# Two MLP products as seven block products each: one step of a hybrid diffusion backbone on one core

## The chip, the cores and the metric

The kernel runs on one core of a Trainium2 chip, and the metric is the device time of one execution in microseconds (us). Its engines run beside each other and meet through semaphores: TensorE (PE, matrix products), VectorE (DVE), ScalarE (ACT), GpSimd (POOL) and SyncE (SP), whose queue issues all the transfers of this kernel. A smaller time is better.

## The reference, cut to what matters

Two layers run over 1152 tokens (1024 of a sample, 128 of a prompt) with 1024 features. Each layer norms and modulates the tokens, projects them, runs a convolution, grouped attention and neighbourhood attention, projects back, and ends with an MLP:

```python
    x = x + g1 * (jnp.concatenate([a_out, b_out, c_out], axis=-1) @ w_out)
    h = _rms(x, n2) * (1 + sc2) + sh2
    x = x + g2 * (jnp.square(jax.nn.relu(h @ w1)) @ w2)
```

`w1` is 1024 x 4096 and `w2` 4096 x 1024. All is float32. `sh`, `sc` and `g` come from a modulation vector, one for the sample's tokens and one for the prompt's, as `silu(c) @ ada_w + ada_b` for each layer.

## The kernel before

Features lie on partitions, tokens along the free axis. Residuals `X[k]` (k = 0 to 7, 128 features each) and the normed activations stay in SBUF. Nothing is ordered by a scheduler: the code is emitted in the order in which it stands (`tc.manual_schedule()`), generators are advanced by hand with `next`, and each engine runs its own instructions strictly in that order. Helpers record most operations, so that many have the line of a helper: L92 is `tt` (tensor_tensor), L95 `stt` (scalar_tensor_tensor), L86 and L89 ACT's activation and copy, L132 a transfer.

**High and low parts.** PE multiplies in fp32r. To keep float32 accuracy every operand is split: `hi` is the value cast by ACT, `lo` is value minus `hi` by DVE or POOL (`split`). A product is then three matmuls, hi*hi, hi*lo and lo*hi, into one PSUM bank (there are eight, tag `p`).

**The MLP (`mlp`).** The 4096 inner features are 32 blocks `f` of 128, taken two at a time in 16 rounds `c`. A round runs the first product for both blocks, first over the first 512 tokens (`mm1`, L1481 to L1483, 512 columns a matmul), then over the other 640 (`mm1_rest`, through `both_parts` at L1351, 320 columns a matmul). The results go through `relu2` and a split, stay in SBUF as `hid`, and the same round multiplies them with the matching rows of `w2` (`mm2`, L1505 to L1507, 512 columns) and adds each result, times the gate, to `X` by one DVE instruction straight from PSUM. The prompt's part of the second product has the tokens as the stationary side (`mm2p`, L1525 to L1527, names `accp`), with `prompt_tail` at the end.

```python
            for k in range(KT):                                                       # mm1
                mm(ps, wh[:, k, :], h[:, k, :], start=(k == 0), stop=False)           # L1481
                mm(ps, wh[:, k, :], lo[:, k, :], start=False, stop=False)             # L1482
                mm(ps, wl[:, k, :], h[:, k, :], start=False, stop=(k == KT - 1))      # L1483
...
            mm2_part(ps, c, si, n, 1)                                                 # mm2
            stt(xs(n, si), ps, g2[:, 0, n:n + 1], xs(n, si), ALU.mult, ALU.add)
```

So a layer's MLP is 768 matmuls of 512 columns and 1536 of 320 in the first product, 1536 + 192 of 512 in the second.

**Around it.** `out_proj` comes ahead. Its norm for the MLP (`norm2`, names `nx`, `h2h`, `h2l`) runs for the first 512 tokens beside the last parts of the output projection, and for the other 640 beside the MLP's first round. `modulation(0, [1, 2])` is spare work of PE beside layer 0's projections (`fill`, names `aw`, `psmod`, L211); `modulation_beside(1)` makes all six sixths of layer 1's modulation on DVE beside layer 0's MLP (names `macc`), with one small PE sum and four transposes for each sixth (L269, L275). In the last round of layer 0 the next layer's first norm begins. In the last layer finished tokens are turned and stored by `put` (L1616).

## Time and profile before

| | |
|---|---|
| three runs | 3103.09 to 3104.21 us, median 3103.54 |
| profiled execution | span 3103.8 us, within those runs |
| PE / DVE / ACT / POOL busy | 96% / 63% / 35% / 23% of the span |
| TensorE clock granted, mean | 0.984 |
| layer 0's MLP | 749.2 to 1583.2 us of the span |
| layer 1's MLP and the outputs | 2274.5 to 3103.8 us |
| bytes moved | 242.10 MB, mean 78 GB/s |

A row of the profile names line, engine, operation and `out<-in` by the program's names, then shapes as partitions x elements; `busy` of a DVE or POOL instruction contains what it waits inside the instruction. Matmuls overlap their neighbours, so the time that one costs is the distance from its start to the next one's start, not its own duration.

### The profile page before, as it was taken

What the parts mean: (1) busy time and instruction counts of PE and PEld (TensorE: products, weight loads), DVE (VectorE), ACT (ScalarE), POOL (GpSimd) and SP (SyncE); (2) the same over time, 40 slices, a digit from 0 to 9 for tenths busy, and PEclk for the clock granted to TensorE, in tenths of its full rate; (3) what the DMA queues carried; (4) which work ended last, traced back from release to release, by engine and by line L of the source; (5) the groups of instructions that cost most, each with busy time, mean ns of one, the idle gap of its engine ahead of it and who ended that gap; (6) DMA issues with size and microseconds to landing.
All of it is one profiled execution on the core that took longest, in us unless ns stands there. A gap on an engine that the chain in (4) does not pass through costs nothing.

```text
span 3103.8 us, 43730 instructions
## 1 busy us (share of the span) xinstructions
PE 2985.8 (96%) x17136; PEld 2460.4 (79%) x17136; DVE 1962.4 (63%) x3547; ACT 1074.5 (35%) x2230; POOL 718.4 (23%) x653
## 2 busy tenths in 40 slices
PE   6998999999999999999999898999999999999999
PEld 4888645888888888888879884468888888888887
DVE  6587787846766666657467977877374444444444
ACT  4334366844221212121252344578252121212121
POOL 3576256312100000000046754452030000000000
PEclk8999999999999999999999899999999999999999
DMA  7467103331312222222133440134211111111111
GB/s 275 115 183 195 59 16 81 86 95 48 102 60 83 78 78 75 82 62 82 43 109 72 107 120 25 40 75 115 62 41 48 35 48 41 41 41 41 41 48 68
DMA packets 317774, 242.10 MB, mean 78 GB/s; under 512 B 110464, under 2 KB 274048, under 8 KB 316544
## 3 DMA queue, kind: packets, MB, share of 16 engines
q1 hardware_dynamic: 317568, 239.31, 26.2%
q8 instruction: 135, 2.21, 0.3%
q14 instruction: 71, 0.58, 0.1%
HBM read 195.74 MB, written 43.52 MB: 77 GB/s over the span
## 4 chain that ended last, share of the span: by engine, by line
PE 80%; DVE 12%; ACT 3%; POOL 2%; DMA 2%; issue 1%; SPq 1%; DVEq 0%; POOLq 0%; ACTq 0%
PE ps L1351 14%; PE ps L1505 7%; PE ps L1507 7%; PE ps L1506 7%; PE ps L1481 4%; PE ps L1483 4%; PE ps L1482 4%; PE psacc L1149 3%; PE pso L1351 3%; PE pspv L1016 2%; PE pspt L1000 2%; PE pst L573 2%; PE pst L572 2%; PE pst L574 2%; DVE cacc L95 2%; PE psst L1163 2%
## 5 line engine op out<-in xcount | busy, mean ns | idle before, releaser
L95 DVE SCALAR_TENSOR_TENSOR X<-ps,mod,X 128x512 f32<-128x512 f32 x512 | 378.6, 748 | 217.3 <-PE ps L1507 215.4
L86 ACT ACTIVATE re<-ps 128x320 f32<-128x320 f32 (+1 forms) x192 | 87.5, 491 | 1125.9 <-PE ps L1483 853.3
L1505 PE MATMUL ps<-hidh,w2h 128*128 128x512 f32 x1024 | 407.6, 398 | 4.6 <-ACT hidh L89 4.1
L1507 PE MATMUL ps<-hidh,w2l 128*128 128x512 f32 x1024 | 405.0, 396 | 1.1 <-DVE w2l L92 1.1
L1506 PE MATMUL ps<-hidl,w2h 128*128 128x512 f32 x1024 | 405.3, 396 | 0.6 <-DVE hidl L92 0.6
L92 DVE TENSOR_TENSOR re<-ps,re 128x320 f32<-128x320 f32 (+1 forms) x192 | 101.1, 554 | 400.7 <-ACT re L86 400.4
L573 PE MATMUL pst<-wl,hh 128*128 128x256 f32 x1040 | 297.8, 286 | 17.3 <-DVE wl L92 17.3
L572 PE MATMUL pst<-wh,hh 128*128 128x256 f32 x1040 | 298.9, 287 | 2.6 <-ACT wh L89 2.6
L574 PE MATMUL pst<-wh,hl 128*128 128x256 f32 x1040 | 296.2, 285 | 0.0
L92 POOL TENSOR_TENSOR nacc<-nacc,nsq 128x512 f32<-128x512 f32 (+1 forms) x36 | 40.1, 1121 | 930.7 <-ACT nsq L86 930.6
L1505 PEld LDWEIGHTS ps<-hidh,w2h 128*128 128x128 f32 x1024 | 193.4, 189 | 52.7 <-ACT hidh L89 5.0
L1351 PE MATMUL ps<-h2l,w1h 128*128 128x320 f32 x1024 | 233.5, 309 | 0.3 <-POOL h2l L92 0.2
L1351 PE MATMUL ps<-h2h,w1h 128*128 128x320 f32 x1024 | 233.7, 309 | 0.0
L1351 PE MATMUL ps<-h2h,w1l 128*128 128x320 f32 x1024 | 232.7, 308 | 0.0
L1507 PEld LDWEIGHTS ps<-hidh,w2l 128*128 128x128 f32 x1024 | 193.6, 189 | 47.7 <-DVE w2l L92 1.9
L1506 PEld LDWEIGHTS ps<-hidl,w2h 128*128 128x128 f32 x1024 | 193.7, 189 | 44.1 <-DVE hidl L92 1.2
L573 PEld LDWEIGHTS pst<-wl,hh 128*128 128x128 f32 x1040 | 201.1, 193 | 18.2 <-DVE wl L92 18.1
L572 PEld LDWEIGHTS pst<-wh,hh 128*128 128x128 f32 x1040 | 201.0, 193 | 12.6 <-PE pst L574 3.5
L1482 PE MATMUL ps<-h2l,w1h 128*128 128x512 f32 x512 | 201.8, 394 | 1.7 <-POOL h2l L92 1.7
L1481 PE MATMUL ps<-h2h,w1h 128*128 128x512 f32 x512 | 202.7, 396 | 0.0
L1483 PE MATMUL ps<-h2h,w1l 128*128 128x512 f32 x512 | 201.7, 394 | 0.0
L574 PEld LDWEIGHTS pst<-wh,hl 128*128 128x128 f32 x1040 | 201.1, 193 | 0.0
(264 smaller groups left out, 6520.9 us busy)
## 6 DMA issues: line engine op xcount, KB each, us to landing
aw<-in_ada_w SPq DMA_DIRECT2D x160, 256.0 KB, 4.3
w1r<-in_mlp_w SPq DMA_DIRECT2D x64, 512.0 KB, 4.1
w2r<-in_mlp_w SPq DMA_DIRECT2D x64, 512.0 KB, 3.6
ddA<-o SPq DMA_DIRECT2D x144, 128.0 KB, 2.3
wr<-in_w_in SPq DMA_DIRECT2D x28, 512.0 KB, 4.1
qd<-ddA SPq DMA_DIRECT2D x48, 256.0 KB, 3.3
kd<-ddA SPq DMA_DIRECT2D x16, 576.0 KB, 4.8
awh<-in_ada_w SPq DMA_DIRECT2D x8, 1024.0 KB, 12.6
```

What stands on the lines that cost most here:

```text
L92: (eng or nc.vector).tensor_tensor(out=out, in0=a, in1=b, op=op)
L95: nc.vector.scalar_tensor_tensor(out=out, in0=a, scalar=s, in1=b, op0=op0, op1=op1)
L572: mm(o, hi, wh, start=(k == 0), stop=False)
L573: mm(o, hi, wl, start=False, stop=False)
L574: mm(o, lo, wh, start=False, stop=(k == KT - 1))
L1351: mm(ps[:, 0:320], x[:, k, :], y[:, k, o:o + 320], start=(k + z == 0), stop=(k == KT - 1 and z == 2))
L1481: mm(ps, wh[:, k, :], h[:, k, :], start=(k == 0), stop=False)
L1482: mm(ps, wh[:, k, :], lo[:, k, :], start=False, stop=False)
L1483: mm(ps, wl[:, k, :], h[:, k, :], start=False, stop=(k == KT - 1))
L1505: mm(ps, wh[:, cs], hh, start=(j == 0), stop=False)
L1506: mm(ps, wh[:, cs], hl, start=False, stop=False)
L1507: mm(ps, wl[:, cs], hh, start=False, stop=(j == 1))
```

## The change

Both products of the MLP are cut into 2 x 2 blocks and made by the seven products of the Winograd form of Strassen's scheme. Tokens are two halves of 576 (512 of the sample and 64 of the prompt), so `X[k]` becomes a tile of 2 x 576 and a separate prompt tile goes away. Every matmul of the MLP and of the output projection has 288 columns, in pairs over two PSUM banks (`three`, L1372).

```diff
+    OPS = ["B11", "B21", "B22", "T1", "T2", "T3", "T4"]
+    ENDS = ("P2", "P4", "P3")
+    PRODUCTS = {"P1": ("A11", "B11"), "P2": ("A12", "B21"), "P3": ("S4", "B22"), "P4": ("A22", "T4"),
+                "P5": ("S1", "T1"), "P6": ("S2", "T2"), "P7": ("S3", "T3")}
...
+    def three(ps, wh, wl, bh, bl, start, stop):
+        for z, (x, y) in enumerate(((wh, bh), (wh, bl), (wl, bh))):
+            for h in range(2):
+                mm(ps[h][:, 0:HH], x, y[:, h * HH:(h + 1) * HH], start=(start and z == 0), stop=(stop and z == 2), skip_group_check=True)
```

**Sums of the activations.** `norm2` norms the first half into the blocks B11 and B21 as before; for the second half it norms, makes T1 to T4 from both halves and splits them (names `HA`/`HF` for the arena that holds them, `hi`, `low`):

```diff
+            tt(x1, x2, x1, ALU.subtract)
+            tt(raw, y2, x1, ALU.subtract)
+            acopy(hi, raw)
+            tt(x2, y2, x2, ALU.subtract, nc.gpsimd)
+            tt(y1, y1, raw, ALU.subtract, nc.gpsimd)
+            tt(lo, raw, f32(hi), ALU.subtract)
...
+            for u, b in enumerate(("T1", "T3") if k < 4 else ("T4", "B22")):
+                parts(b, k % 4, X[k][:, u, :], nc.gpsimd if u else None)
```

The residual is kept in DRAM meanwhile (`dy`).

**First product.** 16 groups g of two blocks of inner features, seven products each of 24 matmuls. `sums1` makes S1 to S4 of the weights (three on POOL, one on DVE). `taken` gathers a product into `ev`: P1 is copied by ACT, P2 squared, and the others added, by DVE out of PSUM; three blocks are squared by `stt`, four differences follow on POOL, and seven blocks of a group go to DRAM (`hd`). The first six products (P1, P2 of groups 0 to 2, `EARLY`) need only the first half of the tokens.

```diff
+                    o, i = {"P6": (u2, s1), "P7": (u3, s1), "P5": (u3, u3), "P4": (s1, s1), "P3": (u2, u2)}[p]
+                    tt(o[:, c], x, i[:, c], ALU.add)
...
+                for o, x, y, b in ((e3[:, 0, :], u2, h11, "T1"), (e3[:, 1, :], u3, e3[:, 0, :], "T2"),
+                                   (e4[:, 0, :], u3, u2, "T3"), (e4[:, 1, :], s1, e3[:, 1, :], "T4")):
+                    tt(o, x, y, ALU.subtract, nc.gpsimd)
+                    stores.append((b, g, o))
...
+        seq = [(g, p) for g in range(EARLY) for p in ("P6", "P7", "P5", "P4", "P3")]
+        seq += [(g, p) for g in range(EARLY, NG) for p in ("P1", "P6", "P2", "P7", "P5", "P4", "P3")]
...
+            prepare(x + 1)
+            prepare(x + 2)
+            product(g, p)
+            keep(3)
+            next(fill, None)
```

**Second product.** It begins when the first is through. Two halves q of the inner features; 112 steps' worth of 24 matmuls, each with one inner block (`ti`, read back from `hd` in pairs, four steps ahead) and 128 x 512 of weights, which lie in the arena that the first product's activations held. The last two products of q = 1 run in two halves of the outputs, 32 steps of 12 matmuls. All eight PSUM banks hold one running product for four blocks of outputs. Each step splits its block and its weights two steps ahead; P2 and P6 make the weight sums on POOL in place.

```diff
+            acopy(hi, e)
+            tt(lo, e, f32(hi), ALU.subtract)
...
+                src = T([512], n="w2s")
+                tt(src, w2("A22", gi), w2("A11", gi), ALU.subtract, nc.gpsimd)
+                a = w2("A12", gi)
+                tt(a, a, src, ALU.subtract, nc.gpsimd)
...
+            if p == "P2":
+                a, b, d = (w2(y, gi) for y in ("A11", "A21", "A22"))
+                tt(a, a, b, ALU.subtract, nc.gpsimd)
+                tt(b, b, d, ALU.add, nc.gpsimd)
...
+            if n % 2 == 0 or p in ENDS:
+                update(ps, X[m][:, t, :], g2, m)
+            else:
...
+                later.append(add_from(X[m][:, t, :], e, m))
```

P1 is added to three blocks of `X` each; these twelve additions (`later`) run two a step after it.

**Modulation.** `modulation_beside(1, (0, 1))` makes two sixths on DVE beside layer 0's first product; the other four become `modulation(1, [1, 2])` on PE beside layer 1's projections, as layer 0 has it.

What stands where on the engines, at three places. First, DVE where the second half's norm ends, in layer 0 before: the other 640 tokens' norm (`nx`, `h2l`) alternates with the first round's additions to `X`.

```order
L95 SCALAR_TENSOR_TENSOR X_7489<-ps_8384,mod_69,X_7489 128x512
L95 SCALAR_TENSOR_TENSOR nx_8448<-X_7868,A_0_71,rstd_8319 128x512
L95 SCALAR_TENSOR_TENSOR nx_8449<-Xp_7276,A_0_71,rstd_8324 128x128
L95 SCALAR_TENSOR_TENSOR nx_8456<-X_7905,A_0_71,rstd_8319 128x512
L95 SCALAR_TENSOR_TENSOR nx_8457<-Xp_7276,A_0_71,rstd_8324 128x128
L95 SCALAR_TENSOR_TENSOR h2l_8365<-nx_8448,mod_69,h2h_8364 128x512
L95 SCALAR_TENSOR_TENSOR h2l_8365<-nx_8449,mod_69,h2h_8364 128x128
```

Now, on DVE at the same place, the splits of the sums (`low`), P2's results (`ev<-psa`) and, from `w1l_8845` on, the weights of the seventh product (P6 of group 0) and the eighth (P7, `w1l_8872`):

```order
L101 TENSOR_TENSOR low_8793<-X_7505,HA 128x576
L101 TENSOR_TENSOR w1r_8706<-w1r_8704,w1r_8706 128x512
L101 TENSOR_TENSOR ev_8738<-psa_8712,ev_8738 128x288
L101 TENSOR_TENSOR ev_8738<-psa_8713,ev_8738 128x288
L101 TENSOR_TENSOR low_8833<-X_7629,HA 128x576
L101 TENSOR_TENSOR low_8838<-X_7755,hi_8632 128x576
L101 TENSOR_TENSOR w1l_8845<-w1S_8799,w1h_8843 128x512
L101 TENSOR_TENSOR low_8847<-X_7883,hi_8632 128x576
L101 TENSOR_TENSOR low_8852<-X_8011,hi_8633 128x576
L101 TENSOR_TENSOR low_8857<-X_8079,hi_8633 128x576
L101 TENSOR_TENSOR w1l_8872<-w1r_8706,w1h_8870 128x512
```

The weights of P6 stand behind the norm, the sums and five splits, and those of P7 behind three more.

Second, DVE inside layer 0's MLP before, beside the modulation: additions to `X` from PSUM with four `macc` between them.

```order
L95 SCALAR_TENSOR_TENSOR X_7278<-ps_9086,mod_69,X_7278 128x512
L95 SCALAR_TENSOR_TENSOR macc_8674<-aw_8782,silc,macc_8674 128x256 x2
L95 SCALAR_TENSOR_TENSOR macc_8675<-aw_8782,silc,macc_8675 128x256 x2
L95 SCALAR_TENSOR_TENSOR X_7282<-ps_9100,mod_69,X_7282 128x512
L95 SCALAR_TENSOR_TENSOR macc_8672<-aw_9084,silc,macc_8672 128x256 x2
```

Now the same four stand in every product of 24 matmuls until the two sixths are done, between a weight split and two or three instructions on `ev`:

```order
L101 TENSOR_TENSOR w1l_9000<-w1S_8992,w1h_8998 128x512
L101 TENSOR_TENSOR ev_8570<-psb_8878,ev_8570 128x288
L101 TENSOR_TENSOR ev_8570<-psb_8879,ev_8570 128x288
L104 SCALAR_TENSOR_TENSOR ev_8570<-ev_8570 128x576
L104 SCALAR_TENSOR_TENSOR macc_8941<-aw_8949,silc,macc_8941 128x256 x2
L104 SCALAR_TENSOR_TENSOR macc_8942<-aw_8949,silc,macc_8942 128x256 x2
L101 TENSOR_TENSOR w1l_9038<-w1r_8864,w1h_9036 128x512
```

An addition from PSUM has become work from SBUF to SBUF for the most part, and POOL, which had nothing there, now has this group's differences.

Third, DVE in the second product, in the steps of P2: the split of a step (`ts`, `w2l`) and two of P1's twelve additions (names `e`), all from SBUF. Before, the second product had the additions from PSUM shown above.

```order
L104 SCALAR_TENSOR_TENSOR X_13092<-e_13212,mod_71,X_13092 128x512
L104 SCALAR_TENSOR_TENSOR X_13092<-e_13212,mod_71,X_13092 128x64
L101 TENSOR_TENSOR ts_13279<-ti_13158,ts_13279 128x576
L101 TENSOR_TENSOR w2l_13283<-HF,w2h_13282 128x512
L104 SCALAR_TENSOR_TENSOR X_13092<-e_13212,mod_71,X_13092 128x512
L104 SCALAR_TENSOR_TENSOR X_13092<-e_13212,mod_71,X_13092 128x64
L104 SCALAR_TENSOR_TENSOR X_12981<-e_13212,mod_71,X_12981 128x512
L104 SCALAR_TENSOR_TENSOR X_12981<-e_13212,mod_71,X_12981 128x64
```

POOL beside it makes the sums of the weights, 16 in a row for P2 and then P6's, held back by nothing but their data:

```order
L101 TENSOR_TENSOR ev_12884<-ev_12695,ev_12883 128x576
L101 TENSOR_TENSOR HF<-HF 128x512 x16
L101 TENSOR_TENSOR w2s_13473<-HF 128x512
L101 TENSOR_TENSOR HF<-HF,w2s_13473 128x512
L101 TENSOR_TENSOR w2s_13507<-HF 128x512
```

Before, POOL stood idle in this part of the MLP.

More of the change, by code (lines that the diff above doesn't have):

```diff
@@ L1370, in half @@
[L1370 to L1382 removed]
+            update(ps, X[n][:, t, :], g1, n)
```

717 lines of the change are left out of this document (408 added, 309 removed).

## The prediction

> **What bounds the kernel now.** I read the page first, for the engines and their slices.
>
> ```profile
> span 3103.8 us, 43730 instructions
> PE 2985.8 (96%) x17136; PEld 2460.4 (79%) x17136; DVE 1962.4 (63%) x3547; ACT 1074.5 (35%) x2230; POOL 718.4 (23%) x653
> ...
> PE   6998999999999999999999898999999999999999
> ...
> DVE  6587787846766666657467977877374444444444
> ...
> POOL 3576256312100000000046754452030000000000
> ```
>
> PE is full nearly everywhere, and least disturbed in the two MLPs (slices 10 to 20 and 30 to 40), where POOL is idle. Then I cut the span into stages: window, length, and busy time of PE, PEld, DVE, ACT, POOL, then clock, DMA share and GB/s.
>
> ```profile
> 749.20:1583.20 834.00, 823.28 (x4119) 699.49 (x4119) 548.13 (x1013) 193.53 (x357) 39.15 (x31) 1.00 0.23 73
> 2274.50:3103.80 829.30, 818.38 (x4118) 703.03 (x4116) 395.29 (x595) 178.01 (x334) 18.64 (x17) 1.00 0.14 44
> 102.50:650.40 547.90, 520.77 (x3687) 393.07 (x3686) 421.45 (x850) 284.11 (x653) 286.07 (x255) 0.98 0.41 110
> 1636.40:2175.50 539.10, 498.85 (x3551) 393.04 (x3550) 425.67 (x841) 283.75 (x654) 287.78 (x255) 0.96 0.32 81
> ```
>
> The MLPs take 834.0 + 829.3 = 1663.3 us and PE idles 10.7 and 10.9 us in them. They are bound by the columns that PE streams, so fewer matmuls are worth their full time as long as the other engines keep up. What a matmul costs is the distance between starts: PE in order of time for 256 and 512 columns, and one piece of the chain for 320.
>
> ```profile
> 303.85 0.28 PE L573 MATMUL pst<-wl,hh 128*128 128x256 f32 x1
> ...
> 305.99 0.28 PE L573 MATMUL pst<-wl,hh 128*128 128x256 f32 x1
> ...
> 922.23 14.03 PE ps L1351 x96
> ...
> 1159.70 0.39 PE L1505 MATMUL ps<-hidh,w2h 128*128 128x512 f32 x1
> ...
> 1164.99 0.39 PE L1507 MATMUL ps<-hidh,w2l 128*128 128x512 f32 x1
> ```
>
> The first two are 18 starts apart (0.119 us), the 320s take 14.03 / 96 = 0.146, the last two are 23 apart (0.230). Time goes with the columns at all three sizes, 0.45 to 0.465 ns each.
>
> **The change, part by part.** *Matmuls.* Before, the two layers have 4992 of 512 columns (768 + 1536 + 192 a layer) and 3072 of 320: 4992 x 0.230 + 3072 x 0.146 = 1597 us. After: 2 layers x 2 products x 16 inner groups x 7 block products x 24 = 10752 of 288. Between the neighbours, 0.119 x 288/256 = 0.134 and 0.146 x 288/320 = 0.1315; I take 0.132, as 320 is measured over 96: 1419. **Gain 178** (156 to 183). The output projection's 1536 matmuls keep their columns.
>
> *What the others now do.* Rows of DVE and POOL by shape (count, busy, mean ns):
>
> ```profile
> L95 DVE SCALAR_TENSOR_TENSOR X<-ps,mod,X 128x512 f32<-128x512 f32 x512 | 378.6, 748 | 217.3 <-PE ps L1507 215.4
> L92 DVE TENSOR_TENSOR hidl<-re,hidh 128x512 fp32r<-128x512 f32 x64 | 44.3, 693 | 44.4 <-ACT hidh L89 44.4
> L92 DVE TENSOR_TENSOR re<-ps,re 128x320 f32<-128x320 f32 x128 | 56.8, 486 | 246.2 <-ACT re L86 246.2
> L95 DVE SCALAR_TENSOR_TENSOR macc<-aw,silc,macc 128x256 f32<-128x256 f32 x336 | 139.9, 480 | 0.0
> L92 POOL TENSOR_TENSOR nacc<-nacc,nsq 128x512 f32<-128x512 f32 x24 | 31.0, 1290 | 925.3 <-ACT nsq L86 925.3
> ...
> 769.38 0.75 DVE L95 SCALAR_TENSOR_TENSOR nx<-X,A,rstd 128x512 f32<-128x512 f32 x1
> 770.04 0.35 DVE L95 SCALAR_TENSOR_TENSOR nx<-Xp,A,rstd 128x128 f32<-128x128 f32 x1
> ```
>
> A queued DVE instruction starts 0.09 us before the end of the one ahead (769.38 + 0.75 against 770.04). So I count, by width, DVE 0.61 (512) and 0.68 (576) for tensor_tensor, 0.66 and 0.73 for stt, 0.86 for an stt of 512 + 64, 0.37 for 288 columns out of PSUM, 0.40 for a macc; POOL 1.29 (512) and 1.44 (576). Now the rows that decide, DVE and POOL at the start of layer 0's MLP, then DVE by form in 769 to 785 us, where POOL is at work:
>
> ```profile
> 749.42 3.06 POOL L92 TENSOR_TENSOR h2l<-nx,h2h 128x512 fp32r<-128x512 f32 x2 [0.34 <-ACT h2h L89]
> 749.55 3.48 DVE L95 SCALAR_TENSOR_TENSOR nx<-X,A,rstd 128x512 f32<-128x512 f32 x2
> 752.95 0.74 DVE L95 SCALAR_TENSOR_TENSOR h2l<-nx,mod,h2h 128x512 fp32r<-128x512 f32 x1
> ...
> L95 DVE SCALAR_TENSOR_TENSOR nx<-X,A,rstd 128x512 f32<-128x512 f32 x6 | 7.1, 1180 | 0.0
> L95 DVE SCALAR_TENSOR_TENSOR X<-ps,mod,X 128x512 f32<-128x512 f32 x4 | 3.0, 741 | 0.0
> ```
>
> DVE from SBUF alone takes 0.74; beside POOL, two take 3.48 while POOL's two take 3.06. They alternate: a pair costs 1.74, against 0.66 + 1.29 = 1.95 in a row. Out of PSUM DVE is untouched (741). So POOL's time adds to DVE's time from SBUF, less about 0.2 a POOL instruction. The Trainium skill, SBUF — State Buffer, section "Who interferes with whom", says that a DVE instruction with two SBUF inputs and a POOL instruction that reads SBUF exclude each other for a whole instruction. The trace agrees but for the 0.2; by the full rule the waits below would come out some 25 us larger.
>
> *The wait for the second half's norm.* Six products (6 x 24 x 0.132 = 19.0 us) cover it. P6's weights stand behind it on DVE. After 7 us for the reciprocal root (a product on PE, two ACT steps, three of DVE) DVE has 8 x 0.86 norm, 12 x 0.68 sums, 5 x 0.68 splits, 2 x 0.61 weights = 19.7, and POOL 11 of 576 and 3 of 512 at 0.2 less = 16.9: P6 at 43.6, 25 late. P7 stands behind three more pairs, 4 more; I take 30 a layer, **60** (40 if POOL falls behind DVE's order, 80 with the rest serial).
>
> *First product's port.* A group has 7 x 24 x 0.132 = 22.2 us of PE; DVE has 8 x 0.61 + 3 x 0.73 = 7.1 from SBUF and 12 x 0.37 = 4.4 from PSUM, POOL 3 + 4 instructions, 9.6, less 1.4: 15.3 to 19.7. It fits. The first three groups have five products, 15.8 us, and 14 to 17.5. Layer 0 adds four macc, 1.6 us, to each of some 32 products: 51 us more over 43 products (136 us of PE), whose own work is 103 to 131. So DVE is 18 to 46 late there; I take 28, and 2 for layer 1: **30** (10 to 60).
>
> *Turn to the second product.* Nothing of it can run before the last of the first: split, cast, first matmul, 4 us. Then eight steps (25.4 us) ask for 8.4 MB of weights, the eight residuals of 0.59 and five pairs of blocks, of which 10.6 MB stand ahead of the ninth step's blocks.
>
> ```profile
> w2r<-in_mlp_w SPq DMA_DIRECT2D x64, 512.0 KB, 3.6
> kd<-ddA SPq DMA_DIRECT2D x16, 576.0 KB, 4.8
> awh<-in_ada_w SPq DMA_DIRECT2D x8, 1024.0 KB, 12.6
> ```
>
> 73 GB/s fill a share of 0.23 in the window above, so full is some 317 GB/s: 33 us against 25.4. 11 a layer, **22** (8 to 44).
>
> *Second product's port.* A step has 3.17 us of PE, DVE 0.68 + 0.61, two steps ahead. P2's steps add two of P1's additions, 1.72; POOL has 32 sums a half, for P2 mostly in P1's window, for P6 partly in P2's. P1: 8 x 1.29 + 16 x 1.09 = 27.8 to 31 of 25.4; P2: 10.3 + 10.3 + 4 of evictions + 8 to 10 of POOL = 33 to 35 of 25.4, 6.3 forgiven by the lead. In q = 0 late weights spread POOL out. I take 2 and 8 a layer, **20** (5 to 50).
>
> *Half steps and the next layer's start.* In the last 32 steps of 1.58 us a pair of blocks is asked for 6.3 us ahead and needs 4.8 (row `kd`) + 1.3: just in time, and layer 0 has the next norm on DVE and POOL beside it. **16** (4 to 35).
>
> *Joins.* PE at the start of layer 1's projections, and at the end of the program:
>
> ```profile
> 1616.53 0.80 PE L311 MATMUL psn<-nacc,ones 128*128 128x128 f32 x2 [3.55 <-DVE nacc L92]
> ...
> 3096.80 0.49 PE L1616 MATMUL psy<-ident,X 128*128 128x128 f32 x3
> ```
>
> The output projection's tail loses a bit of cover (4); `rest_next` now squares and norms 640 tokens at once behind the last product, by the same prices 37 us against 28.6 of PE, where before the norm lost 3.55 (5); eight groups of `put` instead of four come last (4). **13** (4 to 24).
>
> *Modulation.* PE loses four sixths beside layer 0 and gains four in layer 1's projections.
>
> ```profile
> 901.15 0.97 PE psmod L269 x8
> 903.74 0.44 PE psmt L275 x4
> ...
> PE pst L573 <- DVE wl L92: 17.3, 4, 6.6
> ```
>
> 4 x 1.41 = 5.6 off. Layer 0's projections have this work already: PE is busy 520.8 against 498.9 but the stage is only 8.8 longer, since PE waits there anyway (17.3 for `wl` in layer 1). **+3** (-6 to 16).
>
> *Clock.* In layer 0's MLP PE waits once for `hidh`, 2.1 us, and the clock is 0.54 in the window right behind it:
>
> ```profile
> PE ps L1505 <- ACT hidh L89: 2.1, 1, 2.1
> ...
> 768.80:772.40 3.60, 3.30 (x8) 2.41 (x9) 3.60 (x8) 2.21 (x5) 0.00 (x0) 0.54 0.01 2
> ```
>
> That is 1.7 us a wait, for six new waits **10** (4 to 16). The Trainium skill, TensorE: Matmul & The Clock Gate, Part 1, has the clock halved after an idle window of about 3.4 us; here 2.1 sufficed. By the page two of the six would cost nothing, 3 us less.
>
> *What goes.* Of the 1663.3, 1597 are matmuls and 6 x 1.41 = 8.5 modulation; the other 58 are old waits, half clock, norm sums and the 7.0 from the last `put` to the end. All but `put` are counted anew above: **-51**.
>
> Sum: -178 + 60 + 30 + 22 + 20 + 16 + 13 + 3 + 10 - 51 = -55; 3103.8 - 55 = **3049**. The profiled span stands 0.3 above the median, which changes nothing.
>
> **The rivals.** *The shared port binds (slower).* DVE and POOL own no slack in the places above: full ends for the norm (80), layer 0's macc (60), the second product's port (50, and 30 more if POOL runs P6's sums as soon as P2's weights are split) and the half steps (35): 129 more than the forecast, 3178. For it speaks the pair of 1.74 us; against it that a third of DVE's work reads PSUM. It decides once these four cost 180 together instead of 126. It is the lock that the skill's SBUF page describes, taken in full.
>
> *The waits hide.* Half and less: 40, 10, 8, 5 and 4 instead of 148: 2968. For it speaks that in the projections PE stays busy (498.9 of 539.1) beside DVE 425.7 and POOL 287.8; against it that those stages have other PE work to put between.
>
> *Transfers bind the second product.* If a pair lands in 8 us instead of 4.8 (the 1024 KB rows took 12.6 in a full queue), each of 32 pairs of half steps waits 3 us: +96, 3145. Against it: 0.59 MB in 3.17 us is 186 GB/s of 317.
>
> **How the numbers follow.** Forecast 0.60; hidden 0.16, port 0.17, transfers 0.07. The forecast's own terms, not all at one end, reach from 2995 to 3110. Range 2970 to 3145: it takes in most of the hidden case and part of the slower two. 0.2% is 6 us, about what a measurement of this kernel tells from no change. Faster: 0.16 and 0.55 of the forecast, 0.72 with some of the transfers'; same 0.06; slower 0.22.
>
> **What would show it.** L1372 every 0.132 us inside a product; a gap of 25 to 35 us on PE six products into each MLP, ended by DVE `w1l`; DVE without idle time while `macc` lasts, PE waiting for `w1l` or `ev` there, and not in layer 1; PE waiting for `ts` or `w2l` at the ninth step and at P6's first steps; DVE means well above 0.69 where POOL is busy. I am wrong if PE streams 288 columns in over 0.14 us, if the norm's gap is under 15 us, or if P2 and P6 wait over 20 us each.

## The result, and the profile after

| | before | after |
|---|---|---|
| time, median | 3103.32 us (3100.42 to 3104.21, 4 runs) | 3201.88 us (3199.35 to 3210.35, 4 runs) |
| ratio | | 1.0321, 95% interval 1.0306 to 1.0337 |
| profiled span | 3103.8 us | 3197.6 us |

The change made the kernel 3.2% slower; the forecast was 3049 us, and 3201.88 lies above its range. The page after, to be held against the one before (engines, then the 40 slices):

```profile
span 3197.6 us, 53086 instructions
...
PE 2894.0 (91%) x20284; PEld 2575.1 (81%) x20284; DVE 2180.6 (68%) x3907; ACT 1254.6 (39%) x2640; POOL 1302.5 (41%) x1017
...
PE   6999899996688997999988999999967999889999
...
DVE  6586887835799664757675977878356666575676
...
POOL 3576255212534444206135862552125554450510
PEclk7999999998789998999999999999987999999999
```

PE is busy for 92 us less than before and idle for 186 us more, and in the slices that were all nines it now has holes at the start of each MLP, at each turn to the second product and at the end of layer 0. Those places are cut out next: window, length, busy time of PE, PEld, DVE, ACT and POOL, clock, DMA share, GB/s. In layer 0 these are the six cover products (P1 and P2 of the three early groups), the next 15 products (the three groups' other five) and the next 28, both with `macc` beside them, the second product's P1, its P2, P2 of the second half q (the expectations call the halves quarters), and the half steps; then four of the same of layer 1.

```profile
755.60:826.20 70.60, 31.88 (x150) 28.57 (x149) 39.29 (x68) 32.54 (x69) 27.98 (x19) 0.68 0.17 50
826.20:908.00 81.80, 56.47 (x361) 55.45 (x362) 70.24 (x104) 12.29 (x21) 35.57 (x23) 0.79 0.40 126
908.00:1024.30 116.30, 99.26 (x695) 95.20 (x694) 107.09 (x183) 22.75 (x46) 42.23 (x28) 0.93 0.46 151
...
1234.60:1275.20 40.60, 29.81 (x193) 28.90 (x193) 15.79 (x22) 12.31 (x24) 24.53 (x18) 0.88 1.04 395
1275.20:1305.60 30.40, 28.25 (x192) 27.55 (x193) 30.40 (x45) 12.29 (x22) 13.06 (x9) 0.93 0.37 121
1460.30:1493.90 33.60, 27.70 (x194) 25.64 (x193) 32.32 (x43) 13.33 (x25) 19.29 (x13) 1.00 0.25 74
1572.20:1652.50 80.30, 62.59 (x388) 58.71 (x387) 58.46 (x100) 42.44 (x86) 24.54 (x12) 0.89 0.48 149
...
2354.70:2425.30 70.60, 31.05 (x150) 27.74 (x148) 39.20 (x69) 32.66 (x69) 27.95 (x19) 0.69 0.18 56
2425.30:2491.90 66.60, 55.46 (x360) 54.33 (x361) 43.60 (x58) 13.10 (x23) 36.53 (x23) 0.86 0.28 93
2491.90:2580.90 89.00, 89.00 (x675) 89.00 (x674) 58.82 (x96) 20.87 (x44) 44.28 (x28) 1.00 0.43 144
...
3129.00:3185.50 56.50, 55.49 (x419) 54.55 (x418) 41.47 (x88) 29.02 (x64) 6.41 (x2) 1.00 0.55 174
```

The last row but one is the undisturbed state: 672 matmuls of 288 columns in 89.0 us are 0.132 us each, the clock is 1.00, PE has no gap. So a stage's length less 0.132 a matmul is what it loses; I call it "over". For the first row that is 70.6 - 144 x 0.132 = 51.6 us, for the second 34.3 (layer 1: 19.1), for the third 27.6 (layer 1: 0.2). Summed over the two layers:

| term of the forecast | forecast | over, layer 0 + layer 1 |
|---|---|---|
| wait for the second half's norm (six products) | 60 | 51.6 + 51.6 = 103 |
| first product's port and `macc` (43 products) | 30 | 61.9 + 19.3 = 81 |
| turn (rest of the first product, P1) | 22 | 25.6 + 26.4 = 52 |
| second product's port (P2, P6) | 20 | 17.6 + 17.5 = 35 |
| half steps | 16 | 29.6 + 5.7 = 35 |
| clock | 10 | in the rows above |
| sum | 158 | 306 |

The 148 us between the sums are the error of the forecast (3197.6 - 3049 = 149). No single term made it; each of them came out 1.7 to 2.7 times as large. (Of layer 1's 5.7 in the half steps most is work: 34 matmuls of `put`, 4.8 us, run among them.) The waits on PE in the first 70 us and behind them, in order of time (start, us, matmuls, idle time before and what ended it):

```profile
766.95 1.64 PE L1372 MATMUL psa<-HA,w1h 128*128 128x288 f32 x4 [7.68 <-ACT HA L98]
...
772.92 2.39 PE L329 MATMUL psn<-nacc,ones 128*128 128x512 f32 x4 [3.85 <-DVE nacc L101]
...
786.07 1.33 PE L1372 MATMUL psa<-HA,w1h 128*128 128x288 f32 x4 [6.28 <-DVE HF L101]
...
803.27 1.33 PE L1372 MATMUL psa<-HA,w1h 128*128 128x288 f32 x4 [11.28 <-DVE HF L101]
...
812.33 1.33 PE L1372 MATMUL psa<-HA,w1h 128*128 128x288 f32 x4 [3.20 <-DVE HF L101]
...
826.17 1.33 PE L1372 MATMUL psb<-HA,w1h 128*128 128x288 f32 x4 [5.80 <-ACT w1h L98]
```

The wait is not where the forecast put it. Only 5.8 us stand behind the six products (and 2.2 more inside P6, for `w1l`); 32.3 lie inside them. The cover products wait themselves: for the first half's norm (`HA`, 7.7), for the sum of squares of the second half's norm, whose matmuls stand between theirs (`nacc`, 3.9), and three times for `HF`, a write that they do not read (below). The clock comes on top. Behind these waits PE runs at half speed for a while, as in the row of 5.4 us after the 11.3:

```profile
803.30:808.70 5.40, 5.40 (x22) 5.40 (x23) 2.48 (x5) 0.67 (x1) 2.56 (x2) 0.50 0.00 0
```

In the trace 557 of the 288-column matmuls are followed by the next one after 0.24 us instead of 0.132: 60 us, where the forecast had 10 for six waits. There are 126 distances above 0.26 us, 47 of them above 1 us.

### The profile page after: what moved, and what is told of

It is laid out like the page before. It is cut to its first block, busy times and chain, and to the rows that moved or that the text cites. A ratio compares the mean times of both kernels' runs of the same rounds, so it can differ in the third digit from the quotient of the medians.

```text
span 3197.6 us, 53086 instructions
## 1 busy us (share of the span) xinstructions
PE 2894.0 (91%) x20284; PEld 2575.1 (81%) x20284; DVE 2180.6 (68%) x3907; ACT 1254.6 (39%) x2640; POOL 1302.5 (41%) x1017
## 4 chain that ended last, share of the span: by engine, by line
PE 67%; DVE 17%; DMA 4%; ACT 4%; issue 4%; POOL 3%; SPq 1%; DVEq 0%; POOLq 0%; ACTq 0%
PE ps L1372 17%; PE psb L1372 9%; PE psa L1372 6%; PE psc L1372 5%; PE pso L1372 5%; DVE X L104 3%; PE psacc L1171 2%; PE pspv L1038 2%; PE pst L594 2%; PE pst L595 2%; PE pst L596 2%; PE pspt L1022 2%; DVE macc L104 2%; DVE cacc L104 2%; PE psst L1185 1%
## 5 line engine op out<-in xcount | busy, mean ns | idle before, releaser
L1372 PE MATMUL ps<-ts,w2h 128*128 128x288 f32 x3584 | 646.6, 302 | 69.8 <-ACT w2h L98 39.4
L1372 PEld LDWEIGHTS ps<-ts,w2h 128*128 128x128 f32 x3584 | 542.2, 194 | 79.6 <-ACT w2h L98 42.0
L1372 PE MATMUL ps<-ts,w2l 128*128 128x288 f32 x1792 | 393.6, 301 | 5.8 <-DVE w2l L101 5.1
L1372 PEld LDWEIGHTS ps<-ts,w2l 128*128 128x128 f32 x1792 | 296.1, 194 | 9.6 <-DVE w2l L101 9.4
L594 PE MATMUL pst<-wh,HA 128*128 128x256 f32 x1040 | 297.8, 286 | 0.0
L595 PE MATMUL pst<-wl,HA 128*128 128x256 f32 x1040 | 294.2, 283 | 0.0
L596 PE MATMUL pst<-wh,HA 128*128 128x256 f32 x1040 | 293.6, 282 | 0.0
L101 DVE TENSOR_TENSOR ts<-ti,ts 128x576 fp32r<-128x576 f32 x256 | 201.6, 787 | 105.4 <-ACT ts L98 105.3
L1372 PE MATMUL psa<-HA,w1h 128*128 128x288 f32 x1024 | 195.4, 315 | 59.1 <-DVE HF L101 42.4
L1372 PEld LDWEIGHTS psa<-HA,w1h 128*128 128x128 f32 x1024 | 165.1, 206 | 62.5 <-DVE HF L101 43.8
L594 PEld LDWEIGHTS pst<-wh,HA 128*128 128x128 f32 x1040 | 198.4, 191 | 19.2 <-PE pst L596 6.9
L595 PEld LDWEIGHTS pst<-wl,HA 128*128 128x128 f32 x1040 | 198.3, 191 | 0.1
L596 PEld LDWEIGHTS pst<-wh,HA 128*128 128x128 f32 x1040 | 198.4, 191 | 0.0
L1372 PE MATMUL pso<-HA,woh 128*128 128x288 f32 x1024 | 177.4, 295 | 0.0
```

Of the source, the lines that this page charges most:

```text
L101: (eng or nc.vector).tensor_tensor(out=out, in0=a, in1=b, op=op)
L594: mm(o, hi, wh, start=(k == 0), stop=False)
L595: mm(o, hi, wl, start=False, stop=False)
L596: mm(o, lo, wh, start=False, stop=(k == KT - 1))
L1372: mm(ps[h][:, 0:HH], x, y[:, h * HH:(h + 1) * HH], start=(start and z == 0), stop=(stop and z == 2), skip_group_check=True)
```

## The experiments

All of them are edits of the kernel after; ratios are to the kernel before, whose medians beside them were 3102 to 3107 us. The kernel after stands at 1.0321.

**The first half of the wait.** e1 takes away the write that the cover products do not read.

```diff
+        raws = [S([2, HT], n="raw") for _ in range(2)]
         for i in range(4):
...
-            raw = ha(11520, i, HF)
+            raw = raws[i // 2][:, i % 2, :]
```

> T2's unrounded sum goes to a tile of its own instead of the F32 view of the arena. Theory A (the arena's two views are one buffer to the scheduler, so each of products 3 to 6 waits for the newest HF write, which it does not read): the three waits on HF (6.3, 11.3 and 3.2 us) go in both layers, the six products take 40 to 50 us instead of 70.6, and the sums on DVE, which wait for these products' PSUM, end earlier too: 20 to 25 us a layer, total 3150 to 3165. Rival (the length of the norm and of the sums decides, and the products only happen to pause beside it): the six products shrink but the wait for P6's weights grows by as much; the first P6 starts at most 5 to 8 us earlier, total 3185 to 3195.

3177.53 us, ratio 1.0234 (1.0217 to 1.0251). Of the three waits for `HF` none is left; one wait is new (`ev`), and the one for P6's weights has grown from 5.8 to 12.8, in the same window by cause (total us, times, longest):

```profile
PE psb L1372 <- ACT w1h L98: 12.8, 1, 12.8
PE psa L1372 <- ACT ev L98: 9.1, 1, 9.1
```

The six products fell from 70.6 to 60.8 us in both layers. So the shared arena is shown as a cause, but of its 20.8 us 16.1 came back in these two waits; of the 9.8 us that went about half is busy time of PE (26.7 us there instead of 31.9), which runs at half speed behind fewer waits. That the two waits belong to the same chain of sums and splits is argued, not shown. A had the mechanism, the rival most of the size; the total lies between the two.

e4 issues DVE's remainder of a block one block later.

```diff
-            tt(lo, src, f32(hi), ALU.subtract, eng)
+            if held is None:
+                tt(lo, src, f32(hi), ALU.subtract, eng)
+            else:
+                held.append((lo, src, f32(hi)))
...
+                while held and (len(held) > 1 or i == 3):
+                    tt(*held.pop(0), ALU.subtract)
```

> In the first half's second norm DVE's remainder of a block is issued one block later, so that DVE does not sit behind ACT's two steps of the same block. Theory A (a chain of latencies on queues in order): PE's wait for HA inside the first product, 7.7 us, and the 3.9 for nacc shrink to 0 to 4 together, 5 to 8 us a layer, total 3185 to 3192. Rival (DVE and POOL have no time left there): the waits move by less than 2 us, total 3197 to 3205.

3187.67 us, 1.0262 (1.0240 to 1.0285). The six products take 64.3 us instead of 70.6 in both layers, the waits for `HA` and `nacc` 4.7 and 1.6 instead of 8.1 and 3.9. As A expected: queues in order with two ACT steps between two DVE steps, not a lack of time.

e6 has four groups of cover instead of three.

```diff
-EARLY = 3
+EARLY = 4
...
-                e3, e4 = S([2, HT], n="ev"), S([2, HT], n="ev")
-                for o, x, y, b in ((e3[:, 0, :], u2, h11, "T1"), (e3[:, 1, :], u3, e3[:, 0, :], "T2"),
-                                   (e4[:, 0, :], u3, u2, "T3"), (e4[:, 1, :], s1, e3[:, 1, :], "T4")):
+                keep()
+                for o, x, y, b in ((h11, u2, h11, "T1"), (u2, u3, u2, "T3"), (u3, u3, h11, "T2"), (s1, s1, u3, "T4")):
```

> Four groups instead of three run P1 and P2 ahead of the second half's norm, so eight products cover it instead of six (to make room, a group's T1 to T4 are written over its own finished blocks, after these are stored). Theory A (the norm and the sums have a length of their own, 65 to 70 us from the first product on, whatever PE does): the first P6 comes no more than 3 us later than in the kernel after, so the wait shrinks by the 6.3 us of the two products, total 3183 to 3191. Rival (each product's evictions and splits lengthen DVE's chain by as much as the product covers): less than 2 us a layer, total 3194 to 3202.

3186.54 us, 1.0271 (1.0253 to 1.0288). The total is A's, the mechanism is not. P6 of group 0 starts 78.5 us after the start of the first product instead of 70.6, so the two more products of cover moved it by 7.9 where A allowed 3: the cover is 53 over instead of 52, and the wait before it did not shrink. What was gained came behind it, and in layer 1 alone: the first 21 products there are 59.3 over instead of 70.7, while layer 0's whole first product lost as much as before (123 over for 124). In layer 1 every wait before P7 is now the shortest one of the kernel after:

```profile
2439.65 0.67 PE L1372 MATMUL psb<-hi,w1h 128*128 128x288 f32 x2 [0.51 <-DVE ev L101]
2456.45 0.67 PE L1372 MATMUL psb<-hi,w1h 128*128 128x288 f32 x2 [0.51 <-DVE ev L101]
```

e11 adds to e6 the early issue of group 3's and group 0's weights.

```diff
+        M.load1(3, ("A11", "A12"))
...
+            if x == 4:
+                M.sums1(0)
+            if x == 5:
+                M.split1(0, "S2")
+            if x == 6:
+                M.split1(0, "S3")
             for _ in range(2):
                 next(pre, None)
```

> e6_early, and besides group 3's first weights and group 0's sums and splits are issued ahead of the second half's remainders (low) instead of behind them. Theory A (the first P6 and P7 wait for weights that stand behind eight remainders on POOL, 1.9 us each beside DVE): the first P6 and the first P7 come 5 to 9 us earlier a layer, total 3168 to 3178. Rival (P7 needs the remainders themselves, and these now come later): less than 2 us a layer, total 3182 to 3190.

3192.28 us, 1.0275 (1.0259 to 1.0290): no gain on e6. In layer 1 the first P6 comes 4.3 us earlier, but the first P7 then waits 9.5 us for DVE where it waited 0.5, and the 20 products behind the cover are 14.4 over instead of 7.0. The rival: the remainders that now come later are needed as well.

**P7 behind P6.** In layer 1, where no `macc` runs, the 15 products behind the cover are still 19.1 over. The longest waits stand before P7, which accumulates onto the banks of P6, and DVE must have read these. The kernel after (its third group waits 0.5), then e14 (below), then e17, each in layer 1:

```profile
2438.51 0.88 PE L1372 MATMUL psb<-hi,w1h 128*128 128x288 f32 x2 [4.68 <-DVE ev L101]
...
2460.70 0.88 PE L1372 MATMUL psb<-hi,w1h 128*128 128x288 f32 x2 [3.70 <-DVE ev L101]
```

```profile
2362.92 0.88 PE L1372 MATMUL psb<-hi,w1h 128*128 128x288 f32 x2 [3.08 <-DVE ev L101]
2383.78 0.88 PE L1372 MATMUL psb<-hi,w1h 128*128 128x288 f32 x2 [3.08 <-DVE ev L101]
```

```profile
2333.98 0.88 PE L1372 MATMUL psb<-hi,w1h 128*128 128x288 f32 x2 [6.39 <-DVE ev L101]
```

e16 puts the next group's P6 ahead of a group's P3.

```diff
-        seq = [(g, p) for g in range(EARLY) for p in ("P6", "P7", "P5", "P4", "P3")]
+        seq = [(0, "P6")]
+        for g in range(EARLY):
+            seq += [(g, "P7"), (g, "P5"), (g, "P4")]
+            if g + 1 < EARLY:
+                seq.append((g + 1, "P6"))
+            seq.append((g, "P3"))
```

> The kernel after, but the next early group's P6 is issued between a group's P4 and P3, so that from the second early group on another product stands between P6 and P7 (T1 to T4 written over finished blocks, as in e6_early, to make room; three early groups). Theory A (P7 waits for DVE to read P6 out of the banks that it accumulates onto, 3 to 5 us a group): the 15 early products lose 5 to 8 us a layer, total 3180 to 3190. Rival (the wait is for P7's weights or T3's remainder): under 2 us a layer, total 3195 to 3204.

3188.69 us, 1.0280 (1.0263 to 1.0297). The 15 products went from 19.1 to 16.5 over in layer 1 and from 34.3 to 25.1 in layer 0; in layer 1 the waits of the second and third group are gone, the first one's is 5.4. The total is A's, the 5 to 8 us a layer were found in layer 0 alone.

In layer 1 this does not show the order as the cause. e6, which keeps P7 right behind P6, has only 0.5 us there; e16 shares with it that T1 to T4 are written in place. In the kernel after, DVE's read of P6 for the second group itself waits for POOL's differences,

```profile
2460.10 0.82 DVE L101 TENSOR_TENSOR ev<-psb,ev 128x288 f32<-128x288 f32 x2 [4.15 <-POOL ev L101]
```

which points to a tile that these still held; for the first group DVE has splits of `low` and `w1l` ahead of it. Back to back on the same banks is costly only when DVE comes late. Where it does, the order helps: in layer 0, and in e17, where the same edit took out all three waits of 3.1 us that e14 has in layer 1 (e14's DVE makes four differences ahead of the read), and the half clock behind them: its first 49 products are 37.0 over, e14's 52.0.

**Layer 0's modulation.** e3 takes `macc` off DVE, e9 thins it out.

```diff
-        fill = modulation(0, [1, 2])
+        fill = chain(modulation(0, [1, 2]), modulation(1, [0]))
...
-            m = mlp(L, M, out, iter(()) if last else modulation_beside(l + 1, (0, 1)), last)
+            m = mlp(L, M, out, iter(()), last)
```

> The first two sixths of layer 1's modulation are taken from DVE beside layer 0's first product and computed on PE among layer 0's attention (a third of modulation(1), which already exists for the other groups). Theory A (macc holds DVE up beside the group's own work, by the shared port): layer 0's first product goes from 469 to 425 to 430 us, like layer 1's 426; layer 0's attention gets 4 to 15 longer; total 3165 to 3180. Rival (layer 0's first product is long for another reason, such as its residuals or the stores): it stays above 455, total 3190 to 3215.

3172.33 us, 1.0216 (1.0200 to 1.0231). Of the 43 products the first 15 are 18.9 over and the next 28 only 0.1, as in layer 1: 42.9 us were `macc`'s, forecast 28. Layer 0's attention got 17 us longer for it (the MLP begins at 772.6 instead of 755.6), a little more than expected. A.

```diff
-            next(fill, None)
+            if g >= EARLY and x % 2:
+                next(fill, None)
```

> The modulation of layer 1 stays on DVE beside layer 0's first product, but one step of it stands behind every second product, and only from group 3 on, instead of behind every product from the first P6 on; nothing else. Theory A (the place was wrong, not the amount: DVE has 7.1 + 4.4 us of own work in a group's 22 us of PE, so 0.8 more a product is free, and 1.6 more is not, the less beside the five-product groups): layer 0's first product goes from 469 to 425 to 432 us, with no cost elsewhere, total 3155 to 3162. Rival (each macc lengthens the group through the shared port wherever it stands): at least half of the 43 us stays, total 3178 to 3195.

3192.82 us, 1.0281 (1.0264 to 1.0299). Layer 0's first product is 117 over where it was 124: 36 of the 43 us stayed. My theory that half the density is free fell. The groups of `macc` on DVE (count, busy, mean ns of one) in the kernel after from 908 to 1024 us, in e9 from 893 to 1200, and in e18, where POOL is idle, from 960 to 1170:

```profile
L104 DVE SCALAR_TENSOR_TENSOR macc<-aw,silc,macc 128x256 f32<-128x256 f32 x72 | 44.4, 677 | 0.0
```

```profile
L104 DVE SCALAR_TENSOR_TENSOR macc<-aw,silc,macc 128x256 f32<-128x256 f32 x112 | 82.5, 796 | 0.0
```

```profile
L104 DVE SCALAR_TENSOR_TENSOR macc<-aw,silc,macc 128x256 f32<-128x256 f32 x84 | 34.9, 477 | 0.0
```

The forecast took 0.40 us each. Beside POOL's work the times fall into two groups: in the kernel after 89 of 112 take 0.47 on average, as with POOL idle, and 23 take 1.58 (up to 1.67), so those that meet a POOL instruction become 1.1 us longer.

**The turn and the second product.** e2 asks for the first weights and inputs early.

```diff
+            if x == len(seq) - 5:
+                for gi in range(4):
+                    soon[gi] = T([512], n="w2e")
+                    load(soon[gi], I["mlp_w2"][l, 2 * gi * 128:(2 * gi + 1) * 128, 0:512])
...
-                src = w2(r, gi)[:, c]
+                src = soon.pop(gi) if x < 4 else w2(r, gi)[:, c]
```

> The weights and inputs of the second product's first four steps are asked for five products before the end of the first, into tiles outside the arena; before, they stand in the SP queue behind the last group's stores and behind PE's last read of the arena. Theory A (the queue and the arena hold them up): the gap of PE at the turn goes from 9.8 and 11.3 to under 3 us, and the first eight steps, 15.2 and 14.4 over their matmuls, fall to 5 to 8: 15 to 18 a layer, total 3160 to 3172. Rival (8.4 MB in eight steps is too much for the transfers whatever the start): the gap closes and steps 5 to 8 wait for it instead, at most 5 a layer, total 3187 to 3195.

3197.24 us, 1.0292 (1.0277 to 1.0308). The gap of 9.8 closed (the rest of the first product is 0.4 over instead of 10.4), and P1 took 8.0 of it: 23.2 over instead of 15.2. The rival, though more came back than the 5 us that it allowed; its cause shows in the windows behind the turn, and in the longest wait from 1224 to 1274 us:

```profile
1234.00:1244.00 10.00, 8.38 (x64) 8.14 (x62) 3.10 (x4) 0.00 (x0) 8.02 (x6) 1.00 1.04 374
1244.00:1254.00 10.00, 3.92 (x16) 3.92 (x17) 2.63 (x4) 2.39 (x4) 4.57 (x5) 0.56 1.03 379
1254.00:1264.00 10.00, 9.48 (x64) 9.01 (x63) 2.71 (x4) 2.39 (x4) 5.34 (x5) 0.92 1.05 396
1264.00:1274.00 10.00, 3.65 (x24) 3.43 (x23) 5.30 (x9) 5.11 (x11) 5.94 (x5) 0.76 1.03 402
...
ACT ts L98 <- DMA ti<-hd: 35.2, 3, 27.3
```

The DMA share is full for 40 us at 374 to 402 GB/s, 15.5 MB, while DVE is busy for 13.7 of them and ACT for 9.9, and ACT waits for the blocks that are read back. e5 keeps e2's edit and asks later for what is needed later.

```diff
-                    if gi % 2:
-                        for j in (gi - 1, gi):
+                if x in (5, 7, 9, 11):
+                        for j in (x - 5, x - 4):
...
-            if x < 8:
+            if 4 <= x < 12:
+                n = (0, 4, 1, 5, 2, 6, 3, 7)[x - 4]
```

> The early weights and inputs of e2_turn, and besides the eight residuals are asked for at steps 4 to 11 of the second product instead of 0 to 7, and the blocks A12, A21 and A22, in pairs, four steps later than before; nothing is left out. Theory A (the transfers of the first eight steps bind: 8.4 MB of weights, 4.7 of residuals and 2 of inputs at the 370 to 400 GB/s that e2_turn's windows show are 40 us, and the stage has 25): the first eight steps, 22.9 to 23.2 over their matmuls in e2_turn, fall to 2 to 8, total 15 to 20 a layer below e2_turn: 3157 to 3167. Rival (the splits on DVE and POOL's sums hold these steps up): they stay at 15 or more over, or the steps after them grow by what these lose; total 3185 to 3197.

3189.02 us, 1.0280 (1.0262 to 1.0298). P1 fell to 11.7 and 10.1 over, not to A's 2 to 8, and P2 rose from 5.1 to 12.5 and 14.2, as the rival said. In P2's steps DVE adds P1's sums into the residuals beside POOL's sums of weights; e5's additions from 1264 to 1284 us (count, busy, mean ns):

```profile
L104 DVE SCALAR_TENSOR_TENSOR X<-e,mod,X 128x512 f32<-128x512 f32 x6 | 8.7, 1445 | 0.0
L104 DVE SCALAR_TENSOR_TENSOR X<-e,mod,X 128x64 f32<-128x64 f32 x6 | 6.8, 1131 | 0.0
```

Alone the first takes 0.74 and the second, an eighth of the columns, 0.28. Of the 64-column additions in the whole of e5, 52 take 0.28 and 20 take 1.31; of the 512-column ones 54 take 0.74 and 18 take 1.79. Either becomes 1.04 us longer when it meets one of POOL's sums. e10 is e5 with no addition issued while POOL sums, and with the residuals asked for at steps 8 to 15.

```diff
-            if gi != 7:
+            if gi != 7 and p not in ("P2", "P6"):
                 for _ in range(2):
...
+            if 8 <= x < 16:
+                n = x - 8
```

> Like e5_defer, but the residuals are asked for at steps 8 to 15, and no waiting addition (stt into the residual) is issued in P2's and P6's steps, where POOL sums weights; they follow from P7 on. Theory A (in P2 the additions and POOL's sums exclude each other: e5's profile has the stt of 512 at 1.78 instead of 0.74 and that of 64 at 1.31 instead of 0.28): P2, 12.5 and 14.2 over in e5 and 8.2 in the second quarter, falls to 2 to 5 each, P1 stays at 8 to 11, total 3155 to 3168. Rival (POOL's own 32 sums beside the splits are enough to bind): P2 and P6 together lose less than 4 us, total 3180 to 3190.

3151.38 us, 1.0146 (1.0131 to 1.0161), 1.8% of the time before below the kernel after. P2 of the two quarters, to be held against 30.4 and 33.6 us in the kernel after:

```profile
1263.50:1291.70 28.20, 27.99 (x193) 27.80 (x193) 28.20 (x21) 9.90 (x19) 26.27 (x17) 0.91 0.84 313
1445.10:1471.10 26.00, 25.54 (x194) 25.31 (x192) 24.73 (x19) 11.11 (x21) 22.42 (x15) 1.00 0.16 48
```

A, a little beyond its range. Spreading the transfers alone (e5) had given 0.4%; moving the additions alone was not tried in a run. In the second half q, though, no residuals are loaded and e10 differs from e5 by the additions only: there P2 falls from 8.3 over to 0.7 in both layers, so that part is the additions'.

**The half steps.** e7 runs the next layer's start behind the MLP.

```diff
-            send(m, start())
+            send(m, iter(()))
+            run(start())
```

> Layer 1's first norm and its first weights (start()) run behind layer 0's MLP instead of beside its last 32 half steps. Theory A (that work on the in-order queues of ACT, DVE and POOL holds the splits of the half steps up): layer 0's half steps go from 80.3 to 55 to 58 us, like layer 1's 56.4, and the norm, now bare, costs 25 to 45 us; total 3195 to 3220. Rival (the half steps are slow by their transfers or by the halved width): they stay above 70, total 3215 to 3245.

3201.37 us, 1.0318 (1.0300 to 1.0336): the time of the kernel after. Layer 0's half steps end at 1626.8,

```profile
1575.10:1626.80 51.70, 51.52 (x386) 50.88 (x384) 38.78 (x85) 29.48 (x64) 4.38 (x3) 1.00 0.55 165
```

so they lose next to nothing, and the bare start costs what they gained, 29 us. A: the 30 us are the start's, not the transfers'.

**POOL out of the MLPs.** e13 issues all of POOL's work in the MLPs on DVE (`nc.gpsimd` dropped from `norm2`, `sums1`, T1 to T4 and `ready2`, otherwise the kernel after).

> The kernel after with all of POOL's work in the MLPs (remainders and sums of the second norm, sums of W1, T1 to T4, sums of W2) issued on DVE instead. Theory A (the alternation binds: a DVE and a POOL instruction together take 1.95 us, two on DVE 1.3 to 1.5): the first six products go from 70.6 to 55 to 63 us, layer 0's first product from 469 to 425 to 440, P2 of the second product from 33.6 to 27 to 30; total 3120 to 3150. Rival (DVE has no time for it: 7 more sums of 0.61 to 0.68 a group, 4 a pair of steps): DVE is over 90% busy in the first product and PE waits for it there in both layers; total 3200 to 3300.

3183.89 us, 1.0251 (1.0236 to 1.0266). Outside both expectations: a gain of 0.7%, so DVE has the time, but the six products fell only from 70.6 to 68.0, and P2, where the additions still stand, not at all (32.7 and 33.2 us for 30.4 and 33.6). In layer 0's 43 products the loss beyond layer 1's went from 42.6 to 31.5 us. So giving POOL's work to DVE saves 2.6 of the norm's 51.6 us a layer, and about a quarter of `macc`'s price. As DVE then does that work itself, the run does not price the alternation alone.

**Together.** e8 is e1, e3, e4, e5 and e6; e12 is e1, e4, e9, e10 and e11.

> e1_raw, e3_macc, e4_late, e5_defer and e6_early together. If the gains are of different waits and add up (0.0088, 0.0105, 0.0058 of the time before measured, 0.009 and 0.003 expected of the two last): ratio 1.0321 - 0.037 = 0.995, 3080 to 3100. If e1, e4 and e6 shorten the same wait and the longest chain in it stays (DVE's and POOL's sums): 1.000 to 1.008, 3105 to 3130.

3111.26 us, 1.0028 (1.0016 to 1.0040). The single gains add up to 3.42% of the time before, together they are 2.93%: they are mostly different waits. The first 21 products are 43.3 over in layer 1; 70.7 less the 9.4, 6.1 and 11.4 of e1, e4 and e6 would be 43.8.

> e1_raw, e4_late, e9_thin, e10_calm and e11_first together. If their gains add up (0.0088 and 0.0058 of the time before measured, 0.0135, 0.009 and 0.009 expected): ratio 1.0321 - 0.046 = 0.986, 3050 to 3070, faster than before. If the waits of the norm only change their names, as e8_all's 9.1 and 11.5 us before P1 and P7 suggest, 0.992 to 1.000, 3078 to 3105.

3095.57 us, 0.9968 (0.9957 to 0.9979), the first version that is below the kernel before, by 0.3%. The second expectation's number: e9 and e11 gave less than was expected of them.

e14 is e12 without POOL in the MLPs, e15 the same with POOL kept for the second product's weights.

> e12_all2 with all of POOL's work in the MLPs on DVE. Theory A (alternation): first eight products 40 to 30 to 34 us, the five-product groups 73 to 62 to 66, layer 0's modulation at no cost, the rest as it is: total 3030 to 3055. Rival (DVE full): the second product's sums, which wait for blocks out of DRAM, now hold up DVE's queue in order, P1 to P6 grow by 10 or more a quarter: total 3090 to 3130.

> e12_all2 with POOL's work in the norm and the first product on DVE, and POOL still doing the second product's weight sums. Theory A (alternation; in the second product e10_calm has left 3 to 4 us a quarter of it): as e14_all3 within 10 us, 3035 to 3060. If the rival is right for the second product alone: 30 or more below e14_all3.

e14 3071.22 us, 0.9898 (0.9880 to 0.9916); e15 3085.26 us, 0.9937 (0.9922 to 0.9952). The 40 and 73 us that the expectation names are those of the first six products and of the 15 behind them. e14 fell between its two theories, and e15 is 14 us above it instead of within 10. Against e12 the six hardly moved (40.4 to 39.5 in layer 0), contrary to A. Up to its last matmul layer 0's first product is 16 us more over than layer 1's where it was 30, and P1, P2 and P6 of the second product lose 12 us more with POOL (e15) than without it (e14). So in this kernel POOL is not worth its place even there.

e17 is e14 with e16's order, and `macc` at every product in the last groups so that it ends before the turn. e18 is e17 with POOL's part of layer 1's first norm and weights on DVE (`norm_out` with all its blocks in the way "v", `pr.prep()` without `nc.gpsimd`).

> e14_all3 with the order of e16_order for its four early groups, and layer 0's modulation at every product in the last three groups so that it ends before the turn. Theory A: three waits of 3.1 us a layer and their half clock go, and the 6 us before layer 0's second product: total 3040 to 3055. Rival: 3062 to 3080.

> e17_all4 with POOL's part of layer 1's first norm and weights, beside layer 0's half steps, on DVE. Theory A (alternation: DVE's short steps there meet POOL's long ones): the half steps go from 80 to 65 to 72, total 8 to 15 below e17_all4. Rival (DVE and ACT are full: 61 of 85 us busy on DVE, and 15 to 20 more to come): 80 or more, total the same or up to 10 above.

e17 3047.27 us, 0.9817 (0.9803 to 0.9832); e18 3034.79 us, 0.9778 (0.9763 to 0.9792). Both totals as A expected. In e17 the 6 us before layer 0's second product closed, but its P1 took 5.3 of them; the gain is that of the three waits. e18's half steps take 72.3 us where e17's take 80.6:

```profile
1488.10:1560.40 72.30, 60.11 (x388) 56.29 (x388) 56.74 (x109) 39.30 (x82) 9.34 (x3) 0.93 0.54 167
```

e18 is 2.2% faster than the kernel before and 5.2% faster than the kernel after (3034.79 / 3201.88), with the same matmuls.

## Why the prediction was wrong, point by point

*Matmuls, -178: right.* The median distance of the 288-column matmuls is 132 ns in every kernel here, and the row 2491.90:2580.90 shows a stage at exactly that. e18 ends with 69 us of it as time saved.

*Norm, 60: the step that failed first.* It counted DVE's and POOL's work in one line (43.6 us until P6) and took six products of PE as running beside it at their full speed. P6 came after 70.6 us, and 103 was measured. Neither half of the step held: the cover products do not run beside the norm, they wait 32 us a layer for its parts, and DVE and POOL are not through after 43.6. Of the difference of 43 us e1 shows 20 as a wait for an unrelated write in the same arena, and e4 12 as DVE waiting for ACT in order. POOL's share of the rest is small: with its work on DVE 68.0 of the 70.6 us a layer remain (e13). What remains is taken to be a chain DVE, ACT, DVE per block, which another order shortens (e4) and more cover does not (e6). With all edits the eight cover products of e18 still are 29 over a layer; what would be the next link is not settled.

*First product, 28 and 2: too small twice.* Layer 1's 2 were 19.3, since the step compared sums of work with PE's time and left out that P7 needs P6's banks read: DVE reads them late behind splits in its queue, and behind POOL's differences (e6 is free of both waits; the order alone is shown in e17). Layer 0's `macc` was 42.6 and not 28 (e3, e9). That is near the top of the step's own 18 to 46, the end at which DVE's reads out of PSUM hide nothing of POOL's time. A part stays open: in e17 and e18, with POOL idle, layer 0's first product is still 25 us longer than layer 1's, although `macc` now takes 0.48 us.

*Turn, 22: the mechanism right, the size wrong.* 52 was measured. The bytes were underestimated, 10.6 MB ahead of the ninth step's blocks, where the queue of e2 stayed full for 40 us and 15.5 MB; the rate was underestimated as well, 317 GB/s for 374 to 402. And the gap of 9.8 us was not in the sum beyond 4: e2 closes it by asking for the first weights and inputs ahead of the last group's stores and into tiles outside the arena; which of the two it takes is not shown.

*Second product's port, 20: right mechanism, 35.* Here the alternation does bind, as the rival of the shared port had it: e10 takes most of it away by moving twelve additions. The prediction's price of a pair held, for short instructions too: POOL's 1.29 less 0.2 is 1.09 on top of DVE's own time, and 1.04 was measured on 64 and on 512 columns. What it had wrong was how many pairs there are. In P2 of the second half q 13 POOL instructions ran (the row 1460.30:1493.90), 13.5 us at 1.04 each, where it had 8 to 10. In the first half it let late transfers thin them out; there P2 and P6 lost 7.3 us, in the second half 10.3, where I read its "2 and 8" as these two. The Trainium skill, SBUF — State Buffer, "Who interferes with whom", has the port pair that DVE shares with POOL as an exclusive lock, and a DVE instruction with two SBUF inputs as contending for it with a POOL instruction that reads SBUF. The 1.04 us agree but for the 0.25 that POOL's 1.29 has more.

*Half steps, 16 for both: 29.6 and 5.7.* It named the transfers, and for layer 0 the next norm beside them; e7 shows the next layer's start as the whole cause in layer 0, and layer 1, with the same transfers, loses next to nothing beyond `put`'s matmuls.

*Clock, 10: 60.* The price of a wait was about right (60 / 47 = 1.3 us, forecast 1.7); the number of waits was wrong (47 above 1 us, not six). It grew with the other terms, and fell with them: 272 matmuls at half clock in e18, 29 us.

*Joins and modulation, 16: near.* Layer 0's MLP begins 6.4 us later, the stretch between the MLPs is 11 longer, and the end behind the last product takes 12.1 instead of 7.0.

Of the marks that the prediction set, the 0.132 us, DVE nearly full beside `macc` (107.1 of 116.3 us) and DVE's longer means beside POOL came, and so did waits at the ninth step (5.9 us) and at P6's first (1.9), though for P1's copies and the additions out of PSUM and not for `ts` or `w2l`. The gap of 25 to 35 us behind six products did not come: it is 5.8, and a gap under 15 was one of the three signs that were to show the prediction wrong. That sign came, since the wait had moved in among the products; the other two did not. The rivals: "the shared port binds" gave 3178, nearest to the time, and its mark was passed: its four places cost 254, it had 255, the mark was 180. That is luck in the main: 81 of the 254 are the whole first product, and the largest, the norm with 103 for its 80, hardly changes with POOL out of it (e13). The reason holds in the second product and for a part of `macc`. The common fault of the sum is that each term was a balance of work against PE's time with lead and latency left out; five balances that were each almost even all came out on the wrong side.

## What to carry to other kernels

Where fewer matmuls are bought with many small steps on engines in order, ask of each place not whether the work fits but how long the chain of one block is, what stands ahead of it in each queue, and whether the next matmul needs banks that another engine must read first. Two views of one buffer can make an access to one wait for a write to the other that it does not need (e1). Give work to POOL only where DVE has none from SBUF at that time, and count instructions there, not their lengths. When one edit brings two changes (cover and tiles in e6, order and tiles in e16), look in the trace which of them a wait went away with, before the total is taken as proof.

## What the runs showed of the hardware

A DVE instruction from SBUF that meets one of POOL's becomes about 1 us longer whatever its own length: in e5 0.28 us became 1.31 (64 columns) and 0.74 became 1.79 (512 columns), and a `macc` of the kernel after 0.47 became 1.58. So short ones lose the most. Out of PSUM 288 columns took 0.45 with POOL at work and without it (e9 and e14). With POOL's sums moved to DVE the whole became faster (e14 against e12: 0.9898 for 0.9968), although POOL had been a second engine for them.

A product that accumulates onto banks which DVE must read first waits 0.5 us when DVE is there in time (e6, layer 1) and up to 9.6 us when it is not (layer 0 of the kernel after).

The queues reached 402 GB/s at a share of 1.03, a quarter more than the 317 that the rows of before let expect. The Trainium skill, Perfetto Trace Analysis, "Roofline", has one active core of trn2 bounded near 435 GB/s by its 16 DMA engines; the measured rate is under that and agrees.
